# Channel shuffle of 67 MB: two load and two store buffers of 50 KB a partition in place of two and three of 38 KB

## The chip, the core and the metric

The kernel runs on one core of one Trainium2 chip. The metric is the device time of one execution in microseconds (us). Before the change it is 316.12 us, the median of three runs that lie between 316.11 and 316.13 us.

The core has several engines that run side by side, each with its own queue of instructions. Three of them matter here. SyncE (SP) only issues transfers, ScalarE (ACT) here does the same, and VectorE (DVE) copies within the on-chip memory. Transfers are carried out by 16 DMA engines that all queues share. The on-chip memory has 128 partitions; a "tile" is a block with a stretch of bytes in each partition.

## What is computed

```python
def setup_inputs():
    batch, h, w, c = 16, 64, 64, 256
    groups = 8
    ...

def reference(x, groups):
    batch, h, w, c = x.shape
    channels_per_group = c // groups
    x = x.reshape(batch, h, w, groups, channels_per_group)
    x = x.transpose(0, 1, 2, 4, 3)
    x = x.reshape(batch, h, w, c)
    return x.astype(np.float32)
```

There are 16 x 64 x 64 = 65,536 pixels of 256 channels in float32, 1 KB a pixel and 67.1 MB in all. Within each pixel the 256 channels, seen as 8 groups of 32, are transposed to 32 groups of 8. No arithmetic is done. Everything is read once and written once.

## The kernel before

The pixels are split into tiles. A tile of q pixels a partition holds 128 x q pixels in a row, and each partition holds q whole pixels that lie together in memory, so one partition's part is one contiguous run of q KB on both sides of a transfer. This text calls such a run a row. A transfer has 128 rows, 8 for each of the 16 DMA engines.

The list `_SLOTS` (line 12) names the tiles in order. Each entry is one pair of buffers, and the numbers in it are the pieces that share this pair: `[4, 8]` are two pieces of 4 and 8 pixels one behind the other in the first pair, `[28]` fills part of the second, then come twelve tiles of 38 and one of 16 pixels. The sum is 512 pixels a partition, which the assertion in line 30 demands. All buffers have the size of the largest entry (`biggest`, line 31): 38 pixels, 38 KB a partition. The pools (lines 36 and 37) have `_IN_BUFS` = 2 load buffers and `_OUT_BUFS` = 3 store buffers, so 5 x 38 = 190 KB a partition.

The loop from line 45 on goes through the entries. It takes the next load buffer and the next store buffer in turn (lines 46 and 47). Then SP issues the loads of all the entry's pieces (line 55). Then, for each piece, DVE copies it from the load buffer to the store buffer with the channels permuted (line 57), and ACT issues its store (line 61). Each of the three engines works through its own part in program order, and waits are put in by the framework where a buffer is reused or data must be there:

- a load waits until the copy that last read its load buffer is done, that is, the copy of two entries earlier;
- a copy waits for its load, and until the stores that last read its store buffer have landed, that is, those of three entries earlier;
- a store waits for its copy.

SP's loads go through one DMA queue (q1 in the profile) and ACT's stores through another (q10). Nothing else is in these queues. TensorE and GpSimd have no part in the work, apart from four small constants at the start.

Of the kernel before, what the change touches and what calls it, by code (L numbers as in the profile page):

```python
# [1 line left out]

# [4 lines left out]


F32 = mybir.dt.float32
P = 128  # L10

_SLOTS = [[4, 8], [28]] + [[38]] * 12 + [[16]]
_IN_BUFS = 2
_OUT_BUFS = 3


@with_exitstack
def kernel(
    ctx: ExitStack,
    tc: tile.TileContext,  # L20
    x: bass.AP,
    groups: bass.AP,
    out: bass.AP,
):
    nc = tc.nc
    b, h, w, c = x.shape
    G = int(groups)
    CPG = c // G
    assert G * CPG == c
    assert sum(map(sum, _SLOTS)) * P == b * h * w  # L30
    biggest = max(map(sum, _SLOTS))

    x_flat = x.rearrange("b h w c -> (b h w c)")
    out_flat = out.rearrange("b h w c -> (b h w c)")

    in_pool = ctx.enter_context(tc.tile_pool(name="in_pool", bufs=_IN_BUFS))
    out_pool = ctx.enter_context(tc.tile_pool(name="out_pool", bufs=_OUT_BUFS))

    def rows(flat, first, q):

        return flat[first * c : (first + P * q) * c].rearrange("(p f) -> p f", p=P)

    ctx.enter_context(tc.manual_schedule(engines=None))
    first = 0
    for parts in _SLOTS:
        in_tile = in_pool.tile([P, biggest * c], F32, name="in_tile")
        out_tile = out_pool.tile([P, biggest * c], F32, name="out_tile")
        at = 0
        pieces = []
        for q in parts:  # L50
            pieces.append((q, first, slice(at * c, (at + q) * c)))
            first += P * q
            at += q
        for q, start, cols in pieces:
            nc.sync.dma_start(out=in_tile[:, cols], in_=rows(x_flat, start, q))  # L55
        for q, start, cols in pieces:
            nc.vector.tensor_copy(  # L57
                out=out_tile[:, cols].rearrange("p (i j g) -> p i j g", j=CPG, g=G),
                in_=in_tile[:, cols].rearrange("p (i g j) -> p i j g", g=G, j=CPG),
            )  # L60
            nc.scalar.dma_start(
                out=rows(out_flat, start, q), in_=out_tile[:, cols]
            )


# [1 line left out]
_INS = ['x', 'groups']  # L67
_OUTS = [((16, 64, 64, 256), 'float32')]

_NUMBERS = {'groups': 8}  # L70


# [26 lines left out]
```

## Time and profile before

The profiled execution has a span of 314.4 us from its first to its last instruction. The span leaves out what lies around the program, so it is 1.7 us less than the median of the runs.

| what | value |
|---|---|
| median of the runs | 316.12 us |
| span of the profiled execution | 314.4 us |
| copies of 38 pixels | 12, 8.79 us each |
| copies of 28, 16, 8 and 4 pixels | 6.57, 3.87, 2.02 and 1.09 us |
| time that DVE waited | 179.4 us of 314.4 |
| bytes read and written | 67.11 MB and 67.11 MB |
| mean rate over the span | 427 GB/s |
| rate from 94.33 to 278.19 us | 433 GB/s |

Of the profile, these views are used below. The page gives the busy time of each engine and, in 40 equal slices of the span, the busy share of each engine and of the DMA engines in tenths (a 9 is 90% or more). It also lists the DMA queues, with packets and bytes, and groups of DMA issues, with size and median time from issue to landing. The view of the waits says which engine waited for what: total, times, longest. The timeline lists instructions in order of time; start and duration are in us, and the idle time before an instruction stands in square brackets with what ended it. The trace also has a record of each packet that a DMA engine moved: queue, size, start and duration. Here one data packet is one row.

### The profile page before, as it was taken

What the parts mean: (1) busy time and instruction counts of PE and PEld (TensorE: products, weight loads), DVE (VectorE), ACT (ScalarE), POOL (GpSimd) and SP (SyncE); (2) the same over time, 40 slices, a digit from 0 to 9 for tenths busy, and PEclk for the clock granted to TensorE, in tenths of its full rate; (3) what the DMA queues carried; (4) which work ended last, traced back from release to release, by engine and by line L of the source; (5) the groups of instructions that cost most, each with busy time, mean ns of one, the idle gap of its engine ahead of it and who ended that gap; (6) DMA issues with size and microseconds to landing.
All of it is one profiled execution on the core that took longest, in us unless ns stands there. A gap on an engine that the chain in (4) does not pass through costs nothing.

```text
span 314.4 us, 132 instructions
## 1 busy us (share of the span) xinstructions
DVE 119.0 (38%) x16; POOL 0.2 (0%) x4
## 2 busy tenths in 40 slices
DVE  2081907309109109019028028037046055065400
POOL 0000000000000000000000000000000000000000
DMA  7999999999999999999999999999999999999997
GB/s 317 405 441 416 435 416 483 401 465 406 450 421 446 426 436 436 401 470 396 475 396 475 396 470 401 470 401 470 401 450 421 446 426 436 436 417 450 429 421 321
DMA packets 4608, 134.22 MB, mean 427 GB/s; under 512 B 512, under 2 KB 512, under 8 KB 768
## 3 DMA queue, kind: packets, MB, share of 16 engines
q1 hardware_dynamic: 2304, 67.11, 49.8%
q10 hardware_dynamic: 2304, 67.11, 49.4%
HBM read 67.11 MB, written 67.11 MB: 427 GB/s over the span
## 4 chain that ended last, share of the span: by engine, by line
DMA 76%; DVE 19%; issue 0%; SPq 0%; DVEq 0%
DMA in_tile<-in_x_dram 76%; DVE out_tile L57 19%; SPq L55 0%; DVEq L57 0%
## 5 line engine op out<-in xcount | busy, mean ns | idle before, releaser
L57 DVE COPY out_tile<-in_tile 128x9728 f32<-128x9728 f32 (+4 forms) x16 | 119.0, 7440 | 179.4 <-DMA in_tile<-in_x_dram 179.4
L80 POOL MEMSET const-uint8-127<- 128x1 uint8 x1 | 0.1, 103 | 0.0
L80 POOL MEMSET const-bfloat16-1.0<- 128x1 bf16 x1 | 0.1, 102 | 0.0
L80 POOL MEMSET const-float32-1.0<- 128x1 f32 x1 | 0.1, 100 | 0.0
L80 POOL MEMSET const-float32-0.0<- 128x1 f32 x1 | 0.1, 99 | 0.2 <-issue 0.2
## 6 DMA issues: line engine op xcount, KB each, us to landing
in_tile<-in_x_dram SPq DMA_DIRECT2D x12, 4864.0 KB, 37.0
out_dram<-out_tile ACTq DMA_DIRECT2D x12, 4864.0 KB, 42.6
in_tile<-in_x_dram SPq DMA_DIRECT2D x1, 3584.0 KB, 14.7
out_dram<-out_tile ACTq DMA_DIRECT2D x1, 3584.0 KB, 30.9
in_tile<-in_x_dram SPq DMA_DIRECT2D x1, 2048.0 KB, 30.4
out_dram<-out_tile ACTq DMA_DIRECT2D x1, 2048.0 KB, 15.2
in_tile<-in_x_dram SPq DMA_DIRECT2D x1, 1024.0 KB, 5.4
out_dram<-out_tile ACTq DMA_DIRECT2D x1, 1024.0 KB, 25.0
```

The lines of the kernel that those rows point to most:

```text
L57: nc.vector.tensor_copy(out=out_tile[:, cols].rearrange("p (i j g) -> p i j g", j=CPG, g=G), in_=in_tile[:, cols].rearrange("p (i g j) -> ...
L80: nc = _bacc.Bacc("TRN2", target_bir_lowering=False, num_devices=1)
```

## The change

The tiles become larger and fewer, and one store buffer is left out. The first entry holds pieces of 4 and 22 pixels, then come nine tiles of 50 pixels, and 36 pixels are last. The sum is again 26 + 450 + 36 = 512. There are 12 pieces where there were 16. The buffers are of 50 KB a partition, two for loads and two for stores, 200 KB together. A copy now waits for the stores of two entries earlier instead of three.

```diff
-_SLOTS = [[4, 8], [28]] + [[38]] * 12 + [[16]]
+_SLOTS = [[4, 22]] + [[50]] * 9 + [[36]]
 _IN_BUFS = 2
-_OUT_BUFS = 3
+_OUT_BUFS = 2
```

The loop, the order of issue, and the instructions' kinds stay as they are.

## Prediction

> **What bounds the kernel now.** I read the page's busy shares and slices first, then the waits, then the DMA issues, then the timeline.
>
> ```profile
> DVE 119.0 (38%) x16; POOL 0.2 (0%) x4
> DMA  7999999999999999999999999999999999999997
> DMA packets 4608, 134.22 MB, mean 427 GB/s; under 512 B 512, under 2 KB 512, under 8 KB 768
> q1 hardware_dynamic: 2304, 67.11, 49.8%
> q10 hardware_dynamic: 2304, 67.11, 49.4%
> ```
>
> The transfers fill every slice but the first and the last. Loads (q1) and stores (q10) share the same 16 DMA engines half and half. Of 4608 packets, 512 are completion marks (32 transfers on 16 engines), so 4096 are data rows: one row per partition and transfer, 8 rows for each engine in each transfer.
>
> ```profile
> DVE out_tile L57 <- DMA in_tile<-in_x_dram: 179.4, 16, 14.3
> ```
>
> In the waits, every copy waits for a load, never for a store; the copies are hidden, and a copy costs nothing unless the DMA engines run dry during it. The kernel's time is thus head, transfer work and tail, plus any hole. In the records of single packets the first row starts at 1.75 us and the last ends at 313.3 us, so 1.75 + 311.55 + 1.1 = 314.4 us, the span. The median of the runs is 316.12 us, 1.7 us more; I work in span time and add 1.7 us.
>
> ```profile
> 94.33 8.77 DVE L57 COPY out_tile<-in_tile 128x9728 f32<-128x9728 f32 x1 [14.27 <-DMA in_tile<-in_x_dram]
> ...
> 278.19 8.73 DVE L57 COPY out_tile<-in_tile 128x9728 f32<-128x9728 f32 x1 [14.21 <-DMA in_tile<-in_x_dram]
> 286.96 11.83 ACTq L61 DMA_DIRECT2D out_dram<-out_tile  x2
> 294.54 3.87 DVE L57 COPY out_tile<-in_tile 128x4096 f32<-128x4096 f32 x1 [7.62 <-DMA in_tile<-in_x_dram]
> ```
>
> In the timeline the steady period is (278.19 - 94.33) / 8 = 22.98 us for 16 rows of 38 KB on each engine, 1.436 us a row. The last copy ends at 298.4 us.
>
> **What a row costs, and the gain.** In the packet records of the tail, rows of 38 KB start 1.435 us apart and rows of 16 KB 0.607 us apart: 0.828 / 22 = 0.03764 us per KB, and 1.435 - 38 x 0.03764 = 0.005 us per row beside the bytes. By the rows' recorded durations (1.439 and 0.611 us) it is 0.009 us. The bytes stay the same. The change has 12 pieces where there were 16, so 8 transfers and 64 rows per engine fewer: 64 x 0.005 = 0.32 us, or 64 x 0.009 = 0.58 us. Eight completion marks of 0.009 us (their recorded duration) add 0 to 0.07 us. The gain lies between 0.32 and 0.65 us. I take 0.35, because start distances add up to time and durations overlap. New rows: 50 KB 1.887 us, 36 KB 1.360, 22 KB 0.833, 4 KB 0.155.
>
> **Issues and the head.** SP now issues the 4, 22 and 50 pixel loads at once, where it issued 4, 8 and 28. Alone they are 8 x (0.155 + 0.833 + 1.887) = 23.0 us of rows. The next load needs the 22 pixel copy, which ends at about 16.3 us, so the load queue never empties: cost 0. The first row still leaves at 1.75 us. An issue takes 0.33 to 0.43 us on SP or ACT, off the path. SP's and ACT's waits change their times, not their order. Without this cover a late load would cost its own delay.
>
> **Copies.** From 28 pixels (6.57 us) to 38 (8.79 us) a pixel costs 0.222 us: 50 pixels take 11.46 us, 36 pixels 8.35 us, 22 pixels about 5.2 us. During a copy the other load buffer and the other store buffer hold transfers. A 50 KB load alone needs 8 x 1.887 = 15.1 us, more than 11.46, so a full queue covers a copy. If that cover were gone, each of nine copies could expose up to 11.46 us.
>
> **The wait that two store buffers add.** A copy now needs the store before last to have landed; DVE is the engine that would stand, with the next copy behind it and ACT's store and SP's load behind that. The period becomes 16 x 1.887 = 30.2 us, so a store may take 2 x 30.2 - 11.5 = 48.9 us from issue before a copy stands.
>
> ```profile
> in_tile<-in_x_dram SPq DMA_DIRECT2D x12, 4864.0 KB, 37.0
> out_dram<-out_tile ACTq DMA_DIRECT2D x12, 4864.0 KB, 42.6
> out_dram<-out_tile ACTq DMA_DIRECT2D x1, 2048.0 KB, 15.2
> out_dram<-out_tile ACTq DMA_DIRECT2D x1, 512.0 KB, 14.3
> in_tile<-in_x_dram SPq DMA_DIRECT2D x1, 512.0 KB, 3.3
> ```
>
> Stores of 38 KB take 42.6 us: with two buffers of 38 KB they would be late (2 x 22.98 - 8.8 = 37.2), with 50 KB the allowance grows. My estimate for the new store comes from the order of rows. The 512 KB store takes 14.3 us where the same load took 3.3: after 4.0 us of start its eight short rows alternate one by one with load rows of 1.06 us. A completion mark takes a turn too.
>
> The Trainium skill ("DMA: Bandwidth & Descriptors", section "Queues, rings and completion order") says instead that an engine drains a whole packet, typically 9 to 17 descriptors, before it turns to another queue. By that the last 50 KB store would run wholly before or after the last load, with a hole of some 10 us (326 us) or none (315.8 us). The 14.3 us speak for single rows, and I go by them.
>
> Laying out the start in such turns: the 4 KB store, issued at 5.19, has its first row at about 8.5 us (the 1.1 us that the first load took, then the load row in progress and two more, as before) or 9.4 us. The 22 KB load ends near 10.5 us, its store is issued at 16.3. The first 50 KB load lands near 29.6 us, when 3 (or 2) of the 22 KB store's rows are done. Its copy ends at 41.1, and the 22 KB store at about 42.8 us: five rows of 0.833 and five of 1.887 us after that load. So the first large store just finds the queue occupied; were it late it would fall back one or two turns. From here both queues alternate, and each 50 KB load lands with 3, 2 or 1 rows of a store done. A store then takes some 37.5, 41.3 or 45 us. All are under 48.9 us: cost 0, bounds 0 and, were a store 2 us over on each of the last eight copies, still 0 as long as the queues are full.
>
> **The tail, where cover is thin.** Before, the queued 38 KB store's rows end at 298.4 + 15.2 - 0.3 - 8 x 0.607 = 308.4 us; the 16 pixel store needed a place from 298.4 + 1.1 = 299.5 on: 8.9 us to spare. Now the last load is 36 pixels. It lands with 5, 6 or 7 rows of the last 50 KB store left, 9.4, 11.3 or 13.2 us. From its completion to the first row of its store it takes 0.35 (landing) + 0.1 + 8.35 + 0.03 + 1.1 = 9.95 us. The hole is 0.5 us with 5 rows, none with 6 or 7. Unknown is how soon a store starts on an idle queue: from below the first load's 1.1 us, from above the first store's 4.0 us, which would make it 12.85 us and the hole 3.4, 1.5 or 0 us. I take 1.1 us, since the 4.0 were spent behind load rows, and 5 rows: 0.5 us.
>
> The Trainium skill ("DMA: Bandwidth & Descriptors", "Latency and other measured facts") gives about 0.6 us to the first byte of a transfer from SP or ACT. The first load's 1.1 us differs from it; by the page the hole would shrink to nothing and the time be 315.8 us.
>
> **Sum.** 314.4 - 0.35 + 0.5 = 314.55 us of span, and 1.7 us: 316.3 us. Within 0.2% (0.63 us, about what a measurement of this kernel can tell from no change).
>
> **Rivals.**
> 1. Forecast: transfer work as before, tail hole of 0 to 1 us: 315.7 to 316.75 us. Chance 0.45.
> 2. Slower: the last store starts late. One mechanism in one place: behind the 8.35 us copy of the last 36 pixels the store queue runs dry for over 1 us. It decides once the hole passes 0.35 + 0.63 = 0.98 us; with the late start of 4.0 us it is 1.5 or 3.4 us: 317.3 to 319.2 us. For it: 8.9 us to spare before, about none now. Against: a row more left covers it. Chance 0.40, since small shifts of the row order at the start decide it.
> 3. Faster: a row costs the full 0.009 us, marks count, no hole: 316.12 - 0.65 = 315.5 us. For it: the recorded durations. Against: the start distances. Chance 0.15, unforeseen gains included.
> 4. The third store buffer was needed after all, copies stand for stores: the lead of loads is then spent, but as long as stores fill the engines the time stays as in 1. It is part of 1's chance.
>
> The likeliest gives 316.3 us. The forecast's own range is 315.7 to 316.75; the range that leaves out no more than 2 in 10 is 315.6 to 317.9 us. Faster 0.15, same 0.45, slower 0.40.
>
> **What would show it.** Right: a period of about 30.2 us between large copies; copies waiting for loads alone; every slice of DMA at 9 but first and last; a short dip where the last large store ends. Wrong: a DVE wait for a store with idle DMA engines beside it; a period other than 30.2 us (row cost or row splitting); a hole of over 1 us before the last store's rows.

## The result, and the profile after

The changed kernel takes 317.08 us (median; six runs lie between 316.93 and 317.59, and a seventh, of 321.84 us, counts as slow and is left out of the comparison) where the kernel before takes 316.12 us: a ratio of 1.0029, 95% interval 1.0019 to 1.0039. It is slower by about 0.3%, one microsecond. The forecast was 316.3 us with a range of 315.6 to 317.9. The time is inside that range, but outside the forecast's own, 315.7 to 316.75, and the microsecond did not come from where the prediction looked for it.

The page of the changed kernel, with the busy share of the DMA engines in 40 slices and the packets:

```profile
span 315.3 us, 109 instructions
...
DMA  8998999999999999999999999999999999999996
...
DMA packets 3456, 134.22 MB, mean 426 GB/s; under 512 B 384, under 2 KB 384, under 8 KB 640
```

All slices but the first, the fourth and the last are at 9, so the DMA engines are nearly always busy. The data packets are 3456 - 384 = 3072, or 192 rows on each engine, as foreseen. The waits, and from the timeline the first and the last large copies:

```profile
DVE out_tile L57 <- DMA in_tile<-in_x_dram: 182.6, 12, 19.1
```

```profile
11.67 5.26 DVE L57 COPY out_tile<-in_tile 128x5632 f32<-128x5632 f32 x1 [6.45 <-DMA in_tile<-in_x_dram]
29.83 11.56 DVE L57 COPY out_tile<-in_tile 128x12800 f32<-128x12800 f32 x1 [12.90 <-DMA in_tile<-in_x_dram]
53.87 11.43 DVE L57 COPY out_tile<-in_tile 128x12800 f32<-128x12800 f32 x1 [12.48 <-DMA in_tile<-in_x_dram]
...
236.13 11.60 DVE L57 COPY out_tile<-in_tile 128x12800 f32<-128x12800 f32 x1 [19.07 <-DMA in_tile<-in_x_dram]
266.43 11.43 DVE L57 COPY out_tile<-in_tile 128x12800 f32<-128x12800 f32 x1 [18.69 <-DMA in_tile<-in_x_dram]
292.42 8.33 DVE L57 COPY out_tile<-in_tile 128x9216 f32<-128x9216 f32 x1 [14.57 <-DMA in_tile<-in_x_dram]
```

All twelve copies wait for loads, none for a store, although there are only two store buffers. The first large load was placed near 29.6 us, and its copy starts at 29.83. The issues:

```profile
in_tile<-in_x_dram SPq DMA_DIRECT2D x9, 6400.0 KB, 49.0
out_dram<-out_tile ACTq DMA_DIRECT2D x9, 6400.0 KB, 41.3
out_dram<-out_tile ACTq DMA_DIRECT2D x1, 4608.0 KB, 13.7
```

So a store lands 41.3 us after its issue, well within the 48.9 us that it may take. Nothing on these lines explains a loss, nor does the busy share of the DMA engines, which is 0.99 over the last full stretch (the last two numbers are that share and GB/s):

```profile
250.00:300.00 50.00, 19.01 (x2) 0.00 (x0) 1.00 0.99 427
```

It shows in the last microseconds. These are the DMA slices and packets in a window of 4.0 us before the end of the span, of the kernel before and then of the changed one (each character is 0.1 us):

```profile
DMA  9090309390309790309793300000000000000000
DMA packets 80, 1.05 MB, mean 262 GB/s; under 512 B 16, under 2 KB 16, under 8 KB 16
```

```profile
DMA  8999808888000008000000000000000000000000
DMA packets 32, 0.59 MB, mean 147 GB/s; under 512 B 16, under 2 KB 16, under 8 KB 16
```

Here a packet counts where it starts. In the first line the last group of digits is the last row of all 16 engines, within 0.5 us. In the second, 16 of the 32 packets are completion marks and 16 are the last rows: most start in the first microsecond, and the single 8 further on is one row that starts 0.6 us behind all others. One DMA engine is later than all others, and the program ends with it.

This can be followed through the whole run. Each of the 16 engines marks its own end of each transfer, and the trace has the time of each mark. I call the time from the first to the last of the 16 marks of one transfer its spread:

```
                 spread of a transfer, us, landing near
                 76     137    198    259    304    last
kernel before    0.41   0.37*  0.41*  0.44   0.42*  0.42      (* the nearest transfer)
changed kernel   0.38   0.68   1.06   1.50   1.47   1.46
```

In the kernel before, 16 engines keep step all the way. In the changed kernel the slowest falls back bit by bit from about 80 us on. The difference in span, 315.31 - 314.44 = 0.87 us, splits cleanly at the last transfer. The median engine's mark (the ninth of 16) comes at 313.36 us, before at 313.27: 0.09 us. From there to the slowest engine's mark it is 1.14 us, before 0.35: 0.79 us.

Where is this time lost? In the packet records a 50 KB row takes 1.891 us, nearly always. I call a row late that takes over 0.04 us more than is usual for its size. After 50 us, 24 rows of all engines are late, by up to 0.49 us; all are load rows. Nineteen of them belong to a place where two load rows follow each other because the other queue's turn was a store's completion mark (a doubled turn below). In the kernel before there is one late row, of 0.07 us, in the same stretch.

The records do not name the engine, but in the changed kernel a row starts 0.002 to 0.005 us before the end of the one before it on its engine, so that the rows can be strung into 16 chains. The chain that ends last lost 1.31 us after 50 us, in four rows at 106, 167, 207 and 237 us. The next two lost about 0.9 and 0.7 us, and several hardly anything. So the loss is not one engine's alone: some fall back, and the one that fell back most sets the end. No chain regains what it lost: from the start of the row that it has in hand at 50 us to its end each takes 263.41 or 263.42 us plus what its own rows were late.

### The profile page after: what moved, and what is told of

Its sections match the earlier page's. It is cut to its first block, busy times and chain, and to the rows that moved or that the text cites. A ratio compares the mean times of both kernels' runs of the same rounds, so it can differ in the third digit from the quotient of the medians.

```text
span 315.3 us, 109 instructions
## 1 busy us (share of the span) xinstructions
DVE 118.1 (37%) x12; POOL 0.2 (0%) x4
## 2 busy tenths in 40 slices
DMA packets 3456, 134.22 MB, mean 426 GB/s; under 512 B 384, under 2 KB 384, under 8 KB 640
## 4 chain that ended last, share of the span: by engine, by line
DMA 76%; DVE 19%; issue 0%; SPq 0%; DVEq 0%
DMA in_tile<-in_x_dram 76%; DVE out_tile L57 19%; SPq L55 0%; DVEq L57 0%
## 5 line engine op out<-in xcount | busy, mean ns | idle before, releaser
L57 DVE COPY out_tile<-in_tile 128x12800 f32<-128x12800 f32 (+3 forms) x12 | 118.1, 9843 | 182.6 <-DMA in_tile<-in_x_dram 182.6
## 6 DMA issues: line engine op xcount, KB each, us to landing
out_dram<-out_tile ACTq DMA_DIRECT2D x9, 6400.0 KB, 41.3
```

Source lines behind the costliest of these rows:

```text
L57: nc.vector.tensor_copy(out=out_tile[:, cols].rearrange("p (i j g) -> p i j g", j=CPG, g=G), in_=in_tile[:, cols].rearrange("p (i g j) -> ...
```

## The experiments

Theory A: the transfers set the time, the third store buffer and the tail are worth nothing, and the loss is single engines that fall behind. Theory B: the third store buffer was needed. Theory C: the tail behind the larger last copy costs. Ratios are to the kernel before, with their 95% intervals.

### Two store buffers alone

```diff
-_OUT_BUFS = 3
+_OUT_BUFS = 2
```

> The kernel before with two store buffers in place of three, tiles as before. Theory A (the DMA engines never run dry, the time lost lies in load rows that are held up on single engines): copies now wait for stores by about 5.5 us each, because a 38 KB store takes about 37 to 43 us and 37.2 are allowed, but transfers go on under the wait and the time stays at 316.1 us within 0.3. Theory B (the missing third store buffer is what costs): 316.6 us or more.

Measured: 316.12 us, ratio 1.0006 (0.9993 to 1.0018). Its waits:

```profile
DVE out_tile L57 <- DMA out_dram<-out_tile: 169.3, 13, 14.3
DVE out_tile L57 <- DMA in_tile<-in_x_dram: 13.2, 3, 7.7
```

The DMA slices on its page:

```profile
DMA  7999999999999999999999999999999999999996
```

Thirteen of sixteen copies now wait for a store that frees their buffer, and it costs nothing: the load queue has work while a copy stands, so the engines stay full. Theory B falls. A list of waits looks entirely different for two kernels of the same time.

### The tail split

```diff
-_SLOTS = [[4, 22]] + [[50]] * 9 + [[36]]
+_SLOTS = [[4, 22]] + [[50]] * 9 + [[26], [10]]
```

> The changed kernel with its last 36 pixels as 26 and 10. Theory A: the last large store covered the 36 pixel copy, so nothing is to be won: 317.1 us within 0.3, and the spread between the first and the last DMA engine at the end is again about 1.5 us. Theory C (the tail behind the 36 pixel copy costs): 0.5 us or more faster, 316.5 us or less.

Measured: 320.06 us, ratio 1.0125 (1.0112 to 1.0138), far slower, which no theory had expected. The smaller last copy brought no gain, but this time alone does not decide on theory C. What speaks against C is the changed kernel's own trace: on each engine the last store's rows follow those of the store before without a gap. The spread is 2.0 us at 176 us, long before the kernels differ, and 4.1 us before the last store. A falling-behind of this size again explains the time, but its size is not the changed kernel's, and why it was so large in all four runs (319.79 to 320.60 us) is not known. It also delays the last copy, which waits for the slowest engine's part of the load: the median engine marks that load at 304.5 us, the slowest at 308.2. On the median engine the last store therefore starts 1.4 us after the store before has ended. That costs nothing in this kernel, since the slowest engine is busy with the store before until 313.76 us.

### Old first pieces with long rows, new first pieces with short rows

```diff
-_SLOTS = [[4, 22]] + [[50]] * 9 + [[36]]
+_SLOTS = [[4, 8], [28]] + [[50]] * 9 + [[22]]
```

> Tiles of 50 pixels as in the changed kernel, two and two buffers, but the pieces 4, 8 and 28 of the kernel before at the start, and 22 pixels last. If the long rows themselves make single DMA engines fall behind: spread at the end 1 us or more and about 317 us again. If it is where in a load the change from one store to the next falls (set by the first pieces): spread about 0.4 us as before and about 315.9 us. Copies wait for stores here, which by theory A costs nothing.

```diff
-_SLOTS = [[4, 8], [28]] + [[38]] * 12 + [[16]]
+_SLOTS = [[4, 22]] + [[38]] * 12 + [[30]]
```

> The first pieces 4 and 22 of the changed kernel, then twelve tiles of 38 and one of 30 pixels, with two and three buffers as before. If the first pieces decide: the spread grows past 0.7 us though the rows are of 38 KB. If the long rows decide: spread about 0.4 us. In both cases the store before the last leaves too few rows to cover the 30 pixel copy: a hole of about 1 us before the last store, so 316.9 to 317.3 us without spread and near 318 us with it.

Measured: 318.18 us (1.0062, 1.0049 to 1.0076) with 50 pixels, spread 3.1 us, ten of its copies waiting for stores; 316.40 us (1.0018, 0.9998 to 1.0039) with 38 pixels, spread 0.5 us, and not one row late by over 0.04 us after 50 us. The first pieces do not decide; the large tiles do. Single runs far above the rest come with 38 KB too, though seldom: 320.23 us among these eleven, 318.65 among the twelve with two store buffers alone. The hole of about 1 us that was expected behind the 30 pixel copy was small. The window from 302 to 305 us, 0.075 us a character:

```profile
DMA  0000909990900000000000000009990000000000
```

The gap in the digits is mostly one row's length, 1.44 us; in the records the large store's last row ends at 303.96 us on the median engine and the last store's first row starts at 304.08, a hole of 0.12 us. Its issue was at 303.18 us, so a store on an idle queue starts 0.85 to 0.9 us after its issue, not after 1.1 or 4.0.

### The changed kernel again, half rows, 46 and 40 pixels

> The changed kernel again, on the same chip as the three kernels beside it. Theory A (single DMA engines fall behind in transfers with long rows): 317 to 318.5 us, copies waiting for loads alone, and the last completions spread over 1 us or more. If the spread is about 0.4 us here and the time still above 316.7 us, theory A falls.

```diff
-_SLOTS = [[4, 22]] + [[50]] * 9 + [[36]]
+_SLOTS = [[4, 22]] + [[26, 24]] * 9 + [[18, 18]]
```

> The changed kernel with the same four buffers of 50 KB, but each tile of 50 pixels as two pieces of 26 and 24 and the last as 18 and 18: rows of 18 to 26 KB, 21 pieces where there were 12. Theory A: the spread stays near 0.5 us and the time is 316.0 to 316.6 us, in spite of 72 rows more on each engine and direction, which cost about 144 x 0.005 = 0.7 us less than nothing to gain elsewhere. If it is the large buffers (200 KB of the partition in use) and not the rows: spread 1 us or more and 317.5 us or more.

```diff
-_SLOTS = [[4, 22]] + [[50]] * 9 + [[36]]
+_SLOTS = [[4, 22]] + [[46]] * 10 + [[26]]
```

> Ten tiles of 46 pixels after the pieces 4 and 22, and 26 pixels last, two and two buffers: 184 KB in use, less than the 190 KB of the kernel before. If long rows decide: spread about 1 us or more and above 316.7 us. If the use of 200 KB decides: spread about 0.4 us and about 315.9 us.

```diff
-_SLOTS = [[4, 8], [28]] + [[38]] * 12 + [[16]]
+_SLOTS = [[4, 8], [28]] + [[40]] * 11 + [[32]]
```

> The kernel before with tiles of 40 pixels (4, 8; 28; eleven of 40; 32 last), two and three buffers: 200 KB in use, rows of 40 KB. If long rows decide: spread near 0.5 us, 316.0 to 316.3 us. If the use of 200 KB decides: spread 1 us or more and 317 us or more.

Measured: the changed kernel 317.95 us on this chip (1.0052, 1.0023 to 1.0081), single runs from 316.26 to 320.56. With 46 pixels 319.01 us (1.0073, 1.0048 to 1.0098), with 40 pixels 317.42 us (1.0030, 1.0006 to 1.0054), single runs from 316.21 to 319.06. The kernel before, on the same chip between them, lay at 316.04 to 316.44 in 32 of 35 runs. So the larger tiles make a time that scatters, and the single figure of 317.08 us is one draw of it. The kernel with 40 pixels came out as had been said for the use of 200 KB and not as for long rows (spread 1.0 us); that with 46 pixels, in 184 KB, came out as for long rows (2.4 us).

The half rows gave 317.50 us (1.0031, 1.0011 to 1.0051), more than the 316.6 expected, but all twelve runs lie between 317.30 and 317.75, and no row is late by over 0.04 us after 50 us. The spread is not the 0.5 us that was expected: in the bulk it lies between 1.1 and 2.7 us from 34 us on, but it does not grow. The 200 KB in use are thus not what delays rows. Two things account for that microsecond. The kernel has 22 pieces, one more than was counted, so 352 rows on each engine against 256 in the kernel before: by the price of the prediction 96 x 0.005 = 0.5 us. And here the hole in the tail opened. Its window from 307 to 310 us (0.075 us a character):

```profile
DMA  5509599095505009000000000099500000099500
```

The store before the last ends at 308.19 us on the median engine, the last store is issued at 308.12 and starts at 309.02: 0.83 us with nothing to move. It is the predicted mechanism, in another kernel.

### 40 pixels in 160 KB, 25 KB rows in the same transfers, and 36 pixels

```diff
-_OUT_BUFS = 3
+_OUT_BUFS = 2
```

> The kernel with tiles of 40 pixels again, but with two store buffers: 160 KB in use where it was 200 KB. If rows of 40 KB and more are held up: single runs scatter over more than 1 us and the median is about 317.4 us, as with 200 KB. If that kernel was slow for its use of memory: 316.1 us, all runs within 0.3 us.

```diff
-        return flat[first * c : (first + P * q) * c].rearrange("(p f) -> p f", p=P)
+        piece = flat[first * c : (first + P * q) * c]
+        if q == 50:
+            return piece.rearrange("(a p f) -> p a f", a=2, p=P)
+        return piece.rearrange("(p f) -> p f", p=P)
...
+            return cols.rearrange("p (a f) -> p a f", a=2)
```

> The changed kernel with tiles, buffers and transfers as they are, but each transfer of 50 pixels a partition takes its pixels from two blocks in memory, so that it has 256 rows of 25 KB instead of 128 of 50 KB. If the length of a row decides: almost no load row is held up after 50 us, single runs lie within about 0.5 us, and the time is 316.2 to 317.2 us (144 rows more on each engine cost about 0.7 us). If the size of a transfer or of a buffer decides: runs scatter over 2 us or more again, median 318 us or more.

```diff
-_SLOTS = [[4, 8], [28]] + [[38]] * 12 + [[16]]
+_SLOTS = [[4, 8], [28]] + [[36]] * 13 + [[4]]
```

> The kernel before with thirteen tiles of 36 pixels and 4 last, two and three buffers. If rows up to 38 KB pass without delay: all runs within 0.4 us, median 316.1 to 316.4 us. If 38 is a lucky size and not an upper bound: scatter over 1 us and 317 us or more.

Measured: 40 pixels in 160 KB 317.88 us (1.0047, 1.0031 to 1.0062), runs from 316.83 to 318.53, so memory in use is not the cause. 36 pixels 316.27 us (1.0003, 0.9994 to 1.0011), all eleven runs between 316.13 and 316.61, no late row: 38 is no lucky size. The two-block transfers gave 318.23 us (1.0069, 1.0048 to 1.0089), as had been said for the size of a transfer or a buffer, with a spread of 2.4 us. Here 62 of 70 late rows are stores, none of them at a doubled turn, and no store row is later than about 0.2 us: another pattern, and against the row's length as the only cause. It could be the size of a transfer (6.4 MB), so one more kernel told these two apart.

### Long rows in smaller transfers

```diff
-                nc.sync.dma_start(out=in_tile[:, cols], in_=rows(x_flat, start, q))
+            src = rows(x_flat, start, q)
+            step = 2 if q == 50 else 1
+            for h in range(step):
+                nc.sync.dma_start(out=in_tile[h::step, cols], in_=src[h::step, :])
...
+            for h in range(step):
+                nc.scalar.dma_start(out=dst[h::step, :], in_=out_tile[h::step, cols])
```

> The changed kernel, each 50 pixel load and store as two transfers, one for the even and one for the odd partitions: rows stay 50 KB long, a transfer moves 3.2 MB instead of 6.4 MB, copies as they were. If the size of a transfer is what lets single engines fall behind (as the transfers of 6.4 MB with rows of 25 KB suggest): almost no delay in rows after 50 us, all runs within 0.5 us, median 316.0 to 316.8 us. If the length of a row decides: scatter over 1 us and a median of 317.3 us or more.

Measured: 323.56 us (1.0214, 1.0173 to 1.0255), six runs from 321.05 to 325.92; the profiled run is the slowest of them. Its slices on the page, and two stretches of it by windows, where the last two numbers are the DMA engines' busy share and GB/s:

```profile
DMA  8999999999999999999999999999999989999592
```

```profile
250.00:300.00 50.00, 17.49 (x3) 0.00 (x0) 1.00 0.99 429
300.00:324.00 24.00, 5.92 (x1) 0.00 (x0) 1.00 0.55 237
```

All but one slice is full until 300 us, and then almost half of the capacity stands idle: most engines have done their part of the last transfers and wait for the last three, first to let the last copy start and then to end. The spread reaches 10.3 us; at 65 us it was 2.3. Transfers of 3.2 MB do not help; the rows are still of 50 KB, and so are the pieces that are copied. There are twice as many ends of large transfers, and 53 load rows are late after 50 us where there were 24.

### All of it in one table

The profiled runs, with the largest row in the bulk of the work, the spread before the last store, the number of rows late by more than 0.04 us after 50 us, and that run's time above 316.1 us:

```
kernel                     row KB  spread us  late rows  time above 316.1 us
half rows                  26      0.9 *      0          1.6
36 pixels                  36      0.4        0          0.2
before                     38      0.4        1          0.0
two store buffers          38      0.6        2          0.3
new first pieces           38      0.5        0          0.3
40 pixels, 200 KB          40      1.0        6          0.7
40 pixels, 160 KB          40      1.1        5          0.8
46 pixels                  46      2.4        23         1.8
changed kernel             50      1.5        24         1.0
changed kernel again       50      1.8        19         1.1
old first pieces           50      3.1        20         2.6
tail split                 50      4.1        32         3.7
even and odd partitions    50      10.3       67         9.8
25 KB rows, two blocks     25      2.4        70         2.5
```

(* between 1.1 and 2.7 us in the bulk, not grown after 50 us; this kernel's time is explained above.) With long rows, the time above the kernel before is close to the spread less 0.4 us. Between 38 and 40 pixels the late rows become more, from 2 at most to 5 or 6. By row length the last line does not fit. The size of a piece fits all fourteen: up to 38 pixels at most two late rows, from 40 on five to seventy.

## Why the prediction was right and where it was not

**Rows and their price: right.** Row counts were as said. Median marks of the large loads lie (265.17 - 83.76) / 6 = 30.235 us apart; 30.2 had been said. Between 60 and 66 us the rows alternate one by one, load and store, and start 1.887 us apart on an engine, as said. The gain of 0.35 us was not measured apart.

**Head: small miss.** It was put at 0. The first row left 0.11 us later, and rows in the first 50 us were late by 1.34 us on the average of the 16 engines, before by 1.15: together 0.3 us.

**Copies and the wait for two store buffers: right.** 11.46 and 8.35 us had been said for the copies; 11.43 to 11.60 and 8.33 were measured. Of the three values for a store's landing, 37.5, 41.3 and 45 us, the middle one came. That waits for stores would cost nothing, rival 4, was shown by the kernel with two store buffers and 38 pixels.

**Tail: cover right to within half a microsecond, and the hole of 0.5 us did not open.** Six rows of the store before the last were left and not five. The last store was issued at 300.79 us; with the 0.85 to 0.9 us measured above it was ready at about 301.65, and the store before it ended between 301.69 (first engine) and 302.10 us (median). Hardly anything was to spare on the first. Rival 2, the late last store, is therefore not what made the kernel slower, though the half rows show that the mechanism exists.

**The step that failed** is the first sentence on the bound: head, transfer work, tail "plus any hole". It took 16 engines for one. It had the loss of time 0 within the transfer work because rows were taken to have a fixed price; in the changed kernel single load rows cost up to 0.49 us more, 1.31 us in all on the engine that fell back most, and the slowest engine ends the program. That term measured 0.79 us, the part of the loss by which the slowest engine falls further behind the median one. The sum then reads 314.4 - 0.35 + 0.3 + 0 + 0.8 = 315.15, against 315.3 us measured. Late rows on the other engines can be the rest: after 50 us they are 0.33 us on the average engine, before 0.01.

**Where luck helped.** The range reached to 317.9 us for a late last store. That did not come, and something else of about the same size filled its place. On another chip the same kernel had a median of 317.95 us, just outside. And none of the three signs of being wrong appeared: period, waits and tail were as for a right forecast, because no sign looked at single engines.

**What stays open.** That the larger tiles bring the late rows is shown, and that the number of store buffers, memory in use, first pieces and tail are not needed for it. What in the tile does it is not settled. Rows of 25 KB were late in transfers of 6.4 MB, and rows of 50 KB in transfers of 3.2 MB, so neither length of row nor size of transfer is needed; the half rows changed both, and the size of the copy with them. Either may do, or what goes with the larger piece: pieces of 40 pixels or more are what the kernels with many late rows share, and no run changed the copy alone. That the copies disturb the rows while they run is unlikely: of 269 late rows in all fourteen traces 105 overlap a copy, and copies fill 38% of the time. Why it begins between 38 and 40 pixels, why some engines are hit far more than others, and why some late rows are stores (13 of 32 in the kernel with the split tail, 62 of 70 with two blocks) is not known either.

No kernel here beat the one before. With two store buffers it has the same time in 152 KB instead of 190.

## What to carry to other kernels

When transfers fill the time, read not only whether the DMA engines are busy but whether they end together: 16 engines at 99% can hide one that is a microsecond late, and larger tiles that save a third of a microsecond in row costs can lose more there. A changed list of waits proves nothing about time; here 169 us of waits for stores cost nothing. And a last tile has to be small enough that the store before it outlasts its landing, its copy and the 0.9 us until its own store starts.

## What the runs showed that was not expected

Tiles of 40 pixels and more make the time scatter: 316.2 to 319.1 us with 40 pixels on the chip where the kernel before lay within 0.4 us in 32 of 35 runs. In the changed kernel an engine that has fallen behind stays behind to the end. The spread shrinks where the queues run dry, as before the last store of the half rows, where it fell from 0.9 to 0.1 us. And splitting each large transfer into even and odd partitions, with no row added, made a kernel that is about 2% slower than the one before (1.7 to 2.6%). It has twice as many ends of large transfers, where the late rows of the changed kernel were found; that this is the reason was not tried by itself.
